# A DeltaNet scan whose matmuls are held in their written order, with counted bursts of projection matmuls between them

## The chip, the cores and the metric

The kernel runs on one core of one Trainium2 chip. The metric is the device time of one execution in microseconds. The median of the three runs shown of the kernel before is 1650.52 us (1648.81 to 1659.55). The execution that was profiled took 1652.23 us, and its trace spans 1650.5 us.

## What is computed

The reference is a trunk of two layers over 256 context tokens and 256 latent tokens of width 1024. In each layer a normalised input `h` goes through one wide projection, whose columns feed three mixers. They are a gated DeltaNet (A), a short convolution (B) and a neighbourhood attention (C). The mixers are gated, summed and projected, and a gated MLP follows. In the last layer only the latent tokens are carried on. The change lies where A and B meet.

A is a linear recurrence over chunks of 64 tokens, for four heads of width 128 and in both directions. The state of a direction at the end of the context starts its scan over the latent tokens:

```python
def step(S, inp):
    u_i, w_i, qk_i, qd_i, kd_i, gl_i = inp
    v_new = u_i - w_i @ S
    o_i = qd_i @ S + qk_i @ v_new
    S = S * gl_i + kd_i.T @ v_new
    return S, o_i
```

B is `bg * dwconv3(cg * hh)`, where `bg`, `cg` and `hh` are 512 columns each of the wide projection.

## The kernel before, in words

All tokens lie along the free axis: 512 columns in layer 0, and in layer 1 only the 256 latent columns where the context is not needed. A projection of 128 output columns is a sum of 24 matmuls (8 slices of the contraction, 3 products of high and low halves: `hi*hh`, `hi*hl`, `lo*hh`). Its weights are loaded by SP's queue, rounded to the high half by ScalarE (L192, `whi`), and the low half comes from a subtraction on VectorE (L195, `wlo`) or, for 24 tiles of layer 1, from a transfer of a half that was prepared before. The pools of `whi` and `wlo` hold three tiles in layer 0 and four in layer 1 (`WS`, L50).

**What is in a layer around the scan.** First come projections, convolutions and norms of k, v and q. VectorE then inverts small triangular blocks (L717 to L721), transposes the result (`Tl`, `Tf`, L722, L757 to L759), and TensorE completes the inverses with many 32x32 matmuls (`py` L772, `pz` L777), which ScalarE copies out (L773, L778). Then the scan runs: `s` = 0 is the context, `s` = 1 the latent tokens, each with four steps `n`. Both directions are worked together, one in each half of the partitions, and the four heads are worked as two groups of two. A step writes, in this order and each kind for both groups before the next kind:

- `pa<-S` (L888): k times the state; VectorE makes `rr` from it (L889)
- `pa<-wt` (L897): the inverse block times `rr`; ScalarE makes `vn` from it (L899)
- `po<-S` (L914): q times the state, where an output is wanted
- `pS` (L926): `kd` times `vn`; VectorE adds it to the decayed state `Sn` (L931)
- `po<-at` (L937): the second part of the output; VectorE adds it later (L944)

`build` (L824) prepares `wt` and `kd` of the next step on VectorE. The first step of a layer has no state, so it has neither `pa<-S` nor `po<-S`. The last has no `pS`.

**Where the short convolution comes in.** `short_conv` (L786) is a generator: it yields after each of its 288 matmuls (12 projections of 24, L792), and evacuates and convolves between projections. `fill(n)` (L815) advances it by `n * FILL[l][3]` matmuls. It is called after `pa<-S`, after `po<-S`, and, where no output is wanted, once more after `pS` (L890, L919, L950). What is left is written after the scan (L959).

**What sets the order.** The program is traced in written order, and a scheduler then orders each engine's instructions by its own estimate of times: of those that it takes as ready, the one written first goes first, so later work fills waits. `keep_in_program_order` ties an instruction behind the one that was traced just before it on its engine. With `SPIN[l]` = 0 neither the scan's matmuls nor those of `fproj` are tied.

Of the kernel before, what the change touches and what calls it, by code (L numbers as in the profile page):

```python
# [69 lines left out]
SQT, SQ0 = 4, 1  # L70
RQE, OTE, ATE, KDQ, KDC = (0, 0), 1, 0, 0, 0
BRO = (0, 1, 2)
SPIN = (0, 0)
FILL = ((3, 0, 0, 0), (0, 3, 2, 2))
UT = 0
QO = (0, 1)
LOE = ((0, 0, 3, 0), (4, 2, 3, 2))
# [7 lines left out]
def trunk(ctx, tc, xin, cin, cbin, con, par, w_ad0, w_ada, w_in, w_ab, bias, w_p, w_o, w_up, w_dn, out, dbg=None):  # L85
# [312 lines left out]
    for l in range(L):  # L398
# [387 lines left out]
        def short_conv():  # L786
            def fproj(ti):
                hi, lo = win(ti)
                ps = pbank("prj")
                for k in range(KD):  # L790
                    for i, (a, b) in enumerate(((hi, hh), (hi, hl), (lo, hh))):
                        mm = PE.matmul(ps[:, OW], a[:, k, :], b[:, k, NA_], start=k == 0 and i == 0, stop=k == KD - 1 and i == 2)  # L792
                        if in_scan[0]:
                            tc.keep_in_program_order(mm)
                        yield ps

            for i in range(4):
                cg = tmp("cg")
                for ps in fproj(SCT + 3 * i):
                    yield  # L800
                A.copy(cg[:, OW], ps[:, OW])
                for ps in fproj(SCT + 3 * i + 1):
                    yield
                uu = tmp("uu")
                V.tensor_tensor(uu[:, OW], ps[:, OW], cg[:, OW], ALU.mult)
                cv = tmp("cv")
                conv3(cv[:, OW].rearrange("p (s t) -> p s t", t=T), uu, lambda tap: pcol(l, "scc", tap * 4 + i), ns)
                for ps in fproj(SCT + 3 * i + 2):
                    yield
                V.tensor_tensor(y_b[:, i], ps[:, OW], cv[:, OW], ALU.mult)  # L810

        in_scan = [SPIN[l]]
        sc_gen = short_conv()

        def fill(n):  # L815
            for _ in range(n * FILL[l][3]):
                next(sc_gen, None)

        def mm(*a, **k):
            i_ = PE.matmul(*a, **k)  # L820
            if SPIN[l]:
                tc.keep_in_program_order(i_)
# [33 lines left out]
        for s in range(2):  # L856
            for n in range(4):
# [15 lines left out]
                for hs, gs in grp:  # L873
# [11 lines left out]
                    for i, h in enumerate(hs):  # L885
# [3 lines left out]
                        V.scalar_tensor_tensor(rr[:, i], pa[:, col2(i)], egr[:, c0 + h : c0 + h + 1], vpr[:, s, b, h], ALU.mult, ALU.subtract)  # L889
                fill(FILL[l][0])  # L890

# [12 lines left out]
                if want_o:  # L904
                    pos = []
                    for hs, gs in grp:
# [10 lines left out]
                        else:  # L917
                            pos[-1] = (po, None)
                fill(FILL[l][1] if want_o and S is not None else FILL[l][2])  # L919

# [28 lines left out]
                else:  # L949
                    fill(FILL[l][2])  # L950
                if not fin:
# [439 lines left out]
```

## Time and profile before

| | |
|---|---|
| median of three runs | 1650.52 us |
| profiled execution | 1652.23 us |
| its span | 1650.5 us |
| TensorE busy | 1588.7 us, 96% |
| VectorE busy | 1167.6 us, 71% |
| ScalarE busy | 799.6 us, 48% |
| GpSimd busy | 224.6 us, 14% |
| mean granted TensorE clock | 0.981 of full speed |

Ends of matmuls are modelled, so TensorE's busy share also holds short holes between instructions. The distance from one start to the next is the safer reading. The scan of layer 0 lies at about 163 to 226 us, that of layer 1 at about 1147 to 1207 us.

### The profile page before, as it was taken

The page shows a single profiled execution, that of the slowest core. Times are in us where ns is not written, and L with a number is a line of the kernel's source. Part 1 is how long each engine was busy: PE and PEld are TensorE (multiplying, and loading weights), DVE is VectorE, ACT ScalarE, POOL GpSimd, SP SyncE. Part 2 cuts the span into 40 slices and gives each one's busy share as a digit, 9 for nine tenths or more (in the row PEclk, how much of TensorE's full clock was granted, in tenths as well). Part 3 has the DMA queues.
Part 4 walks back from the last instruction along what each step waited for, and adds up shares of the span by engine and source line. Part 5 has one row for each costly group of instructions (what it writes and reads, how often), then busy time and mean ns, then how long its engine had stood idle before and what let it go on. Part 6 is the DMA issues. An engine that isn't in the chain of part 4 may idle for free. (4 is left out here: it accounts for less than half of the span.)

```text
span 1650.5 us, 26543 instructions
## 1 busy us (share of the span) xinstructions
PE 1588.7 (96%) x10184; PEld 1362.4 (83%) x10184; DVE 1167.6 (71%) x2311; ACT 799.6 (48%) x1409; POOL 224.6 (14%) x197
## 2 busy tenths in 40 slices
PE   5999999999799999999999999999999999999997
PEld 4677788877588888888888888788798899999997
DVE  3697763678788886878888776586757755677753
ACT  3764442656433333544444223574357554566653
POOL 0100310010000000000000000100332023334442
PEclk9998999999899999999999999997999999999999
DMA  9221012311676674365656876454134156645653
GB/s 372 78 65 52 27 39 90 109 61 43 199 239 230 235 238 139 115 204 178 207 184 195 279 251 203 176 174 171 52 99 128 56 181 183 188 152 181 188 172 112
DMA packets 75824, 257.80 MB, mean 156 GB/s; under 512 B 8433, under 2 KB 9841, under 8 KB 75569
## 3 DMA queue, kind: packets, MB, share of 16 engines
q1 hardware_dynamic: 71360, 239.37, 44.6%
q0 software_dynamic: 4336, 16.74, 2.8%
q8 instruction: 80, 1.31, 0.3%
q14 instruction: 48, 0.39, 0.1%
HBM read 242.44 MB, written 13.63 MB: 155 GB/s over the span
## 5 line engine op out<-in xcount | busy, mean ns | idle before, releaser
L192 ACT CAST whi<-wr 128x1024 fp32r<-128x1024 f32 (+2 forms) x312 | 288.2, 927 | 432.6 <-PE prj L206 99.7
L195 DVE TENSOR_TENSOR wlo<-wr,whi 128x512 fp32r<-128x512 f32 (+2 forms) x324 | 273.0, 859 | 124.2 <-ACT whi L192 118.8
L205 PE MATMUL prj<-hh,whi 128*128 128x512 f32 (+1 forms) x736 | 260.1, 353 | 5.2 <-ACT whi L192 2.0
L207 PE MATMUL prj<-hh,wlo 128*128 128x512 f32 (+1 forms) x736 | 260.0, 353 | 4.2 <-DVE wlo L195 4.2
L206 PE MATMUL prj<-hl,whi 128*128 128x512 f32 (+1 forms) x736 | 259.0, 352 | 0.0
L205 PE MATMUL pup<-hh,whi 128*128 128x256 f32 (+1 forms) x720 | 240.0, 335 | 1.4 <-ACT hh L370 1.4
L206 PE MATMUL pup<-hl,whi 128*128 128x256 f32 (+1 forms) x720 | 239.6, 334 | 0.0
L207 PE MATMUL pup<-hh,wlo 128*128 128x256 f32 (+1 forms) x720 | 239.5, 334 | 0.0
L195 POOL TENSOR_TENSOR wlo<-wr,whi 128x1024 fp32r<-128x1024 f32 (+2 forms) x72 | 142.7, 1983 | 300.4 <-ACT whi L192 289.6
L271 DVE SCALAR_TENSOR_TENSOR aprod<-araw,cb 128x1024 bf16<-128x1024 f32 x128 | 153.8, 1219 | 24.9 <-DMA araw<-w_ada 24.7
L205 PEld LDWEIGHTS prj<-hh,whi 128*128 128x128 f32 x736 | 139.7, 190 | 25.7 <-ACT whi L192 2.8
L207 PEld LDWEIGHTS prj<-hh,wlo 128*128 128x128 f32 x736 | 139.6, 190 | 23.7 <-DVE wlo L195 5.0
L206 PEld LDWEIGHTS prj<-hl,whi 128*128 128x128 f32 x736 | 139.6, 190 | 18.0 <-issue 1.9
L205 PEld LDWEIGHTS pup<-hh,whi 128*128 128x128 f32 x720 | 137.8, 192 | 15.1 <-ACT hh L370 2.0
L207 PEld LDWEIGHTS pup<-hh,wlo 128*128 128x128 f32 x720 | 137.7, 192 | 13.2
L206 PEld LDWEIGHTS pup<-hl,whi 128*128 128x128 f32 x720 | 137.5, 192 | 12.9
L206 PE MATMUL pdn<-fl,whi 128*128 128x256 f32 (+1 forms) x330 | 109.8, 333 | 0.0
L205 PE MATMUL pdn<-fh,whi 128*128 128x256 f32 (+1 forms) x330 | 109.7, 332 | 0.0
L207 PE MATMUL pdn<-fh,wlo 128*128 128x256 f32 (+1 forms) x330 | 109.7, 332 | 0.0
L164 POOL DMA_DIRECT2D lod<-araw x24 | 12.8, 532 | 520.8 <-DVE araw L162 520.8
L380 DVE SCALAR_TENSOR_TENSOR u<-pup,par,u 128x510 f32<-128x510 f32 (+1 forms) x88 | 53.6, 612 | 36.4 <-ACT u L379 36.4
L792 PE MATMUL prj<-hh,whi 128*128 128x512 f32 (+1 forms) x192 | 69.9, 364 | 0.0
(348 smaller groups left out, 3249.7 us busy)
## 6 DMA issues: line engine op xcount, KB each, us to landing
wr<-w_in SPq DMA_DIRECT2D x128, 512.0 KB, 4.1
wr<-w_up SPq DMA_DIRECT2D x88, 512.0 KB, 3.9
araw<-w_ada SPq DMA_DIRECT2D x80, 512.0 KB, 4.3
wr<-w_dn SPq DMA_DIRECT2D x32, 512.0 KB, 4.2
wr<-w_p SPq DMA_DIRECT2D x48, 256.0 KB, 2.9
araw<-w_in SPq DMA_DIRECT2D x24, 512.0 KB, 3.6
lod<-araw POOLq DMA_DIRECT2D x24, 512.0 KB, 3.2
wlo<-lod SPq DMA_DIRECT2D x24, 512.0 KB, 4.2
```

What stands on the lines that cost most here:

```text
L164: G.dma_start(lod[ti], raw)
L192: A.copy(hi[:, c], raw[:, c])
L195: E_.tensor_tensor(lo[:, c], raw[:, c], hi[:, c].bitcast(F32), ALU.subtract)
L205: PE.matmul(ps, hi[:, i, :], xh[:, i, n], start=first and i == 0, stop=False)
L206: PE.matmul(ps, hi[:, i, :], xl[:, i, n], start=False, stop=False)
L207: mm = PE.matmul(ps, lo[:, i, :], xh[:, i, n], start=False, stop=last and i == k - 1)
L271: V.scalar_tensor_tensor(prod, nxt, 1.0, cb[0][:, i], ALU.mult, ALU.mult, accum_out=macc[:, i, b : b + 1])
L380: V.scalar_tensor_tensor(dst[:, :, 1:T], pv[:, :, 0 : T - 1], wc(0), dst[:, :, 1:T], ALU.mult, ALU.add)
L792: mm = PE.matmul(ps[:, OW], a[:, k, :], b[:, k, NA_], start=k == 0 and i == 0, stop=k == KD - 1 and i == 2)
```

## The change

Both entries of `SPIN` become 1: the scan's matmuls (`mm`, L819) and those projection matmuls that `fill` draws while the scan is written (L793) are each tied behind the matmul traced before them. Those that are drawn after the scan stay free. `FILL` gets new counts: in layer 0 a step draws 2 x 3 = 6 projections after `pa<-S` and 1 x 3 = 3 after `po<-S` (or in its place). In layer 1 it draws 3 x 3 = 9 after `pa<-S`, then 2 x 3 = 6 twice in a context step, and 1 x 3 = 3 in a latent step.

```diff
-SPIN = (0, 0)
-FILL = ((3, 0, 0, 0), (0, 3, 2, 2))
+SPIN = (1, 1)
+FILL = ((2, 1, 1, 3), (3, 1, 2, 3))
```

## Rows read from the trace of the kernel before

**Rows 1.** The page, busy time of each engine.
```profile
PE 1588.7 (96%) x10184; PEld 1362.4 (83%) x10184; DVE 1167.6 (71%) x2311; ACT 799.6 (48%) x1409; POOL 224.6 (14%) x197
```

**Rows 2.** Windows, layer 0: stretch, length, busy and count per engine, clock, DMA.
```profile
125.60:163.20 37.60, 37.11 (x407) 26.99 (x405) 28.66 (x66) 15.28 (x23) 0.00 (x0) 0.89 0.13 39
172.40:221.60 49.20, 47.91 (x403) 36.09 (x402) 39.84 (x109) 24.97 (x66) 16.06 (x26) 1.00 0.04 12
226.50:268.30 41.80, 41.80 (x186) 34.61 (x186) 19.70 (x26) 11.69 (x15) 1.43 (x2) 1.00 0.27 88
```

**Rows 3.** Windows of L792 alone: before, in and after each scan.
```profile
125.60:163.20 37.60, 21.57 (x74) 14.09 (x73) 0.89 0.13 39
163.20:226.50 63.30, 13.67 (x31) 6.54 (x31) 0.96 0.08 24
226.50:268.30 41.80, 41.80 (x184) 34.42 (x184) 1.00 0.27 88
1109.50:1147.50 38.00, 20.75 (x150) 19.19 (x150) 0.83 0.61 212
1147.50:1207.00 59.50, 18.77 (x72) 12.16 (x72) 0.97 0.14 45
1207.00:1215.00 8.00, 7.96 (x66) 7.98 (x66) 1.00 0.06 7
```

**Rows 4.** The timeline of VectorE, layer 0 before the scan.
```profile
135.48 1.22 DVE L195 TENSOR_TENSOR wlo<-wr,whi 128x1024 fp32r<-128x1024 f32 x1
...
140.87 0.17 DVE L576 COPY cols<-psst 128x16 f32<-128x16 f32 x1 [0.86 <-PE psst L573]
...
160.21 1.23 DVE L195 TENSOR_TENSOR wlo<-wr,whi 128x1024 fp32r<-128x1024 f32 x1
```

**Rows 5.** The timeline of TensorE, layer 0 before the scan.
```profile
151.71 0.80 PE L792 MATMUL prj<-hh,whi 128*128 128x512 f32 x1
...
154.99 2.01 PE L772 MATMUL py<-ax,X 32*32 32x32 f32 x61
...
160.70 0.80 PE L792 MATMUL prj<-hl,whi 128*128 128x512 f32 x1
```

**Rows 6.** The chain that ended last, layer 1 before the scan.
```profile
1125.44 1.63 PE prj L792 x12
...
1135.37 2.00 PE prj L792 x8
...
1145.29 0.51 PE prj L792
```

**Rows 7.** The timeline of TensorE in the scan of layer 0.
```profile
172.44 0.66 PE L820 MATMUL pa<-S,k__507 128*64 128x128 f32 x8
...
181.03 0.50 PE L792 MATMUL prj<-hh,whi 128*128 128x512 f32 x1
181.46 0.66 PE L820 MATMUL pa<-S,k__507 128*64 128x128 f32 x8
181.94 0.60 PE L820 MATMUL po<-S,q__501 128*64 128x128 f32 x6
...
185.33 1.77 PE L820 MATMUL pS<-vn,kd 64*128 64x128 f32 x14
187.04 1.16 PE L820 MATMUL po<-vn,at 128*128 128x128 f32 x8
188.13 0.66 PE L820 MATMUL pa<-S,k__507 128*64 128x128 f32 x8
...
221.62 0.66 PE L820 MATMUL pa<-S,k__507 128*64 128x128 f32 x8
```

**Rows 8.** The timeline of TensorE, starts of steps in the scan of layer 1.
```profile
1154.63 0.44 PE L820 MATMUL pa<-S,k__9172 128*64 128x128 f32 x4
...
1177.72 0.54 PE L820 MATMUL pa<-S,k__9172 128*64 128x128 f32 x5
...
1202.12 0.44 PE L820 MATMUL pa<-S,k__9172 128*64 128x128 f32 x4
```

## The prediction

> **What bounds the kernel now.** I read the busy shares first: TensorE is busy for 96% of the span and nothing else comes near [rows 1]. So a matmul costs nothing only where TensorE would wait, and the question is where such places are and what fills them. The windows by stage show it. After the scan of layer 0, TensorE is busy for all of 41.80 us, VectorE for less than half [rows 2]: what is added there lengthens the kernel. Before the scan TensorE also looks full, but the windows of line 792 alone show that 21.57 of its 37.11 busy us are short-convolution projections, work written later that was moved up. What is left there is a chain: VectorE's block inverses and transposes, TensorE's `py` and `pz`, ScalarE's copies.
>
> So I count where the 288 projection matmuls of each layer run [rows 3]. In layer 0, 74 lie before the scan, 31 in it and 184 after it (one straddles two windows). In layer 1 it is 150, 72 and 66. The ones before the scan are almost free now. In the scan the timeline shows steps of about 8 us in which lone projections stand between the scan's matmuls [rows 7].
>
> **What the change does to these places.** The tie is to the matmul traced just before, so the first tied projection stands behind the last `pz`, and the others behind the scan's matmuls. Thus 72 matmuls of layer 0 (8 steps of 9) and 132 of layer 1 (4 x 21 and 4 x 12) can no longer run before the scan. Could the free ones written later take their place? Their weights need a place among three (layer 0) or four (layer 1) tiles, and the first three or four projections, written first, hold them until the scan uses them. The trace agrees that three are prepared ahead: the third `wlo` of these runs at 135.48, the fourth only at 160.21, after the first had been used [rows 4]. So I take the stretch before the scan as empty of projections.
>
> **Term 1, after the scan.** Layer 0 keeps 288 - 72 = 216 there instead of 184: 32 more at 41.80/184 = 0.227 us [rows 3] are **+7.3 us**. Layer 1 keeps 156 instead of 66: 90 at 7.96/66 = 0.121 us are **+10.9 us**. Nothing hides this, as TensorE is full there.
>
> **Term 2, before the scan.** The projections that leave also stood in the way. In layer 0 seven of them run from 151.71 to 154.99 ahead of the third `py`, 3.3 us, and another takes 0.8 before the last `pz` [rows 5]. VectorE waits 0.86 us for `psst`, which projections delay [rows 4]. Sum 5.0. In layer 1 the chain itself runs through 1.63, 2.00 and 0.51 us of them [rows 6], sum 4.1. I take the whole, **-9.1 us**. Late next would be what these matmuls wait for themselves (copies by ScalarE), so the other end is 0.
>
> **Term 3, the scan.** For a step in written order I add prices from one step [rows 7]. `pa<-S` has 16 records; eight take 0.48 (181.46 to 181.94), so 0.96, and the same for `po<-S`. `pS`: 14 in 1.71, so 1.95 for 16. `po<-at`: 1.09 for 8, and I give `pa<-wt`, of the same shape, the same. That is 6.05 us. Nine projections at 0.227 are 2.04. A lone projection between half-width matmuls holds TensorE for 0.43 (181.03 to 181.46), 0.2 more than in a stream; I charge that 0.2 once per burst, two bursts, 0.4. Sum **8.5 us**, where the six middle steps now take (221.62 - 172.44)/6 = 8.2: +1.8. The first step now takes 9.2 (163.2 to 172.44). Projections there run at 0.47 each (3.28/7, half clock), nine are 4.2, and with 1.09, 1.95, 1.09 and 0.4 it is 8.7: -0.5. The last lacks `pS`, 6.55 against 226.5 - 221.62 = 4.9: +1.7. Layer 0: **+3.0 us**.
>
> Layer 1: a context step is 0.96 + 1.09 + 1.95 + 21 x 0.121 + 3 x 0.2 = 7.1, against (1177.72 - 1154.63)/3 = 7.7 [rows 8]: three save 1.7. A latent step is 6.05 + 12 x 0.121 + 0.4 = 7.9 against 8.1: three save 0.7. The first adds 0.2 (nine projections at twice 0.121), the last 1.1 (5.95 against 4.9). Layer 1: **-1.1 us**.
>
> Why no further stall: the six or nine projections behind `pa<-S` cover `rr`, `po<-S` with the three behind it covers `vn`, and `po<-at` covers the last add into the state. If that cover is too thin, what follows in written order waits with it, as nothing tied may pass; that is rival A. VectorE is busy 39.84 of 49.2 us in the middle steps [rows 2], 6.6 of 8.2 per step, so it stays below 8.5. Bounds for a step: 0.6 less (the 0.2 per burst gone and `pa<-wt` 0.2 cheaper), or 1.0 more (rival A). I take the sum, being nearest to rows of the same matmuls.
>
> **Two things of no or unknown cost.** `fill` also moves the evacuations (L801 to L810) and the weight loads on SP's queue later, with the matmuls that they serve. SP is no bound: DMA shares are 0.04 to 0.28 in these stretches [rows 2]. ScalarE is busy for half. I cost them at nothing; if a weight load is late, a burst waits and the scan with it, up to one load per projection, again rival A.
>
> The clock: the granted clock is 0.89 in the stretch before the scan of layer 0 and 0.83 in layer 1 [rows 3], with projections keeping TensorE at work. Without them it may stay at the lower level (1.2 GHz) for the `pss`, `psst` and `gram` matmuls. I take 0 and keep as the other end 2 us per layer, an estimate from the 0.86 us that VectorE now waits for `psst`, doubled and rounded up. The Trainium skill (TensorE: Matmul & The Clock Gate, "Part 1: The HAM clock gate") says that the gate's default is the halved rate and that activity releases it. That speaks against the change; by it the sum would be the one with the 4 us.
>
> **The sum.** 7.3 + 10.9 - 9.1 + 3.0 - 1.1 = **+11.0 us** on the profiled execution's 1652.2: 1663.2. That execution lies 1.7 above the median, so I forecast **1662 us**, which is +0.7% on 1650.5. A measurement of this kernel tells about 1% (16.5 us) from no change.
>
> **Rivals.**
> A, *the tied scan stalls* (slower). VectorE or ScalarE issues something long ahead of `rr`, `vn` or a state add, such as a `wlo` of 1.23 us [rows 4] that itself waits for its `whi`. Before, TensorE took another matmul in that time; now all behind waits. At 1.0 us in each of 14 middle and edge steps it is +14: 1676. It decides from about 0.4 us per step, where the total passes 1%. For it: VectorE has only 1.9 us to spare per step. Against: the order kind by kind leaves cover at each wait.
>
> B, *the stretch before the scan stays full*. If the free projections do get places, term 1 (18.2) and term 2 (-9.1) both vanish: 1652.2 + 1.9, less 1.7, is 1652. For it: the scheduler's order is not seen in the trace. Against: the three `wlo` ahead.
>
> C, *the changes of shape are the loss*. Steps are 0.6 us shorter than my sum, 14 x 0.6 = 8.4: 1653. With B as well, and with nothing stalled, 1644. The lone projection's 0.43 against 0.227 speaks for it. The Trainium skill (TensorEngine Tiling (Array Packing), "Key Properties") has as a rule that changing the tiling mode drains the engine. By that rule sorting the kinds is worth more than I charge, and the total would be C's; the trace agrees that a change costs 0.2, but much of that is already in the steps that I compare with.
>
> D, *the change doesn't bind*: free projections still slip between the tied matmuls, so the bursts are longer or broken, and the scan takes as long as now with the rest unchanged: 1651. Against: ties hold by construction; only what is free can slip in.
>
> **Chances.** Forecast 0.45, A 0.27, B 0.10, C 0.13, D 0.05. The forecast's own range is 1655 to 1671 (term 2 at half, the clock's 4). Slower by over 1% (above 1667): most of A and a seventh of the forecast, 0.29. Faster by over 1% (below 1634) would need B, C and more, 0.08. Within 1%: 0.63. The range 1646 to 1678 holds all but the far ends of A and of B with C.
>
> **What would show it.** Right: no line-792 matmul between the last k, v, q work and the last `pz`, except after it; about 216 and 156 of them after the scans; steps near 8.5, 7.1 and 7.9 us; the scans starting 5 and 4 us earlier within their layers. Wrong: line-792 matmuls before the scan as now (B); TensorE idle inside the scan put down to VectorE or ScalarE (A); steps below 8 us with nine projections (C). The prediction falls if the projections lost before the scan are found somewhere that costs nothing.

## The result: 6% slower, and the profile after

The changed kernel takes 1748.15 us (median of six runs, 1742.75 to 1759.73) against 1650.42 us: a ratio of 1.0597 (95% interval 1.057 to 1.0624). The forecast was 1662 us with a range up to 1678, so it was wrong by far, on the side of rival A. The profiled execution is the slowest of the six, 1759.73 us. Its span is 1757.9 us, 107.4 us longer than before, where the medians differ by 97.7.

The page first: the busy line and the row of granted clocks in 40 slices.

```profile
PE 1641.7 (93%) x10184; PEld 1396.3 (79%) x10184; DVE 1169.0 (66%) x2311; ACT 801.5 (46%) x1409; POOL 228.7 (13%) x197
...
PEclk9997569999989999999999999986779999999999
```

The counts are those of [rows 1]; VectorE and ScalarE do the same work in the same time. TensorE alone is busy for 53 us more, and the clock is low in two places, slices 4 to 6 and 27 to 30. These are the two scans with the stretches just ahead of them. The windows of line 792 alone, cut before, in and after each scan, answer to [rows 3] (length, TensorE busy and count, weight loads, clock, DMA):

```profile
126.00:160.00 34.00, 0.00 (x0) 0.00 (x0) 0.64 0.08 25
160.00:287.00 127.00, 48.00 (x128) 27.53 (x128) 0.71 0.05 15
287.00:324.20 37.20, 36.55 (x161) 29.96 (x160) 1.00 0.34 107
1165.70:1197.80 32.10, 0.00 (x0) 0.00 (x0) 0.57 0.16 56
1197.80:1305.50 107.70, 31.99 (x149) 26.37 (x149) 0.69 0.15 49
1305.50:1322.80 17.30, 16.84 (x139) 16.73 (x139) 1.00 0.66 220
```

No projection runs before a scan any more, as forecast. But the scans now take 127 and 108 us where they took 63.3 and 59.5 [rows 3], at a mean clock of 0.71 and 0.69. The waits of TensorE say for what it sat idle (us in total, times, longest):

```profile
PE pa L820 <- ACT vn L899: 13.6, 24, 1.1
PE pa L820 <- DVE rr L889: 11.0, 24, 0.5
...
PE po L820 <- ACT oacc L915: 3.8, 8, 0.5
PE po L820 <- ACT ot L915: 2.9, 6, 0.5
```

None of these rows is in the profile before, but for one wait of 0.4 us. A context step of layer 1 at the full clock, in TensorE's timeline, shows where they sit (the bracket is idle time before the row, and its releaser):

```profile
1222.87 0.44 PE L820 MATMUL pa<-S,k__9172 128*64 128x128 f32 x4
1223.76 0.66 PE L820 MATMUL pa<-S,k__9172 128*64 128x128 f32 x8 [0.46 <-DVE rr L889]
1224.91 0.44 PE L820 MATMUL pa<-S,k__9172 128*64 128x128 f32 x4 [0.49 <-DVE rr L889]
...
1226.46 0.38 PE L820 MATMUL pa<-rr,wt 128*128 128x128 f32 x2
1227.94 0.71 PE L820 MATMUL pa<-rr,wt 128*128 128x128 f32 x4 [1.10 <-ACT vn L899]
1229.17 0.49 PE L820 MATMUL pa<-rr,wt 128*128 128x128 f32 x2 [0.52 <-ACT vn L899]
...
1233.33 0.44 PE L820 MATMUL pa<-S,k__9172 128*64 128x128 f32 x4
```

Four records are one head. Head 0 runs, then TensorE waits until VectorE has made `rr` of head 0; heads 1 and 2 run together, and head 3 waits for the `rr` of head 2. Heads 0 and 1 write into one bank of the accumulation memory, and so do 2 and 3. Between the two, the code has the evacuation of the first, that is, the read that takes its result out of the bank. VectorE's own timeline has that read from 1223.35, for 0.35 us, and head 1 starts at 1223.76. Head 0 needs about 0.24 us of issue, and head 1 starts 0.89 after it. `pa<-wt` has the same two waits for `vn`, and `po<-S` for `ot`: four waits in a context step of layer 1, six in every step with an output. The one of 1.10 us is longer because ScalarE, until 1227.54, still worked off a `whi` (1.05 us from 1226.18) and a `cv` that were issued ahead of `vn`.

The Trainium skill (PSUM — Partial Sum Buffer, "PSUM bank collisions raise a hardware error") says that two engines may not touch one bank in the same partitions at once, even at different columns, and that this must be guarded by semaphores. The waits in the trace fit that: the two heads write different columns, and yet the second starts only after the read of the first has ended (1223.70, then 1223.76).

In the steps with outputs the clock is low as well. Windows of all engines:

```profile
180.00:190.00 10.00, 9.10 (x45) 6.87 (x44) 4.39 (x11) 0.81 (x2) 2.78 (x4) 0.50 0.00 0
260.00:270.00 10.00, 10.00 (x65) 6.79 (x63) 3.29 (x7) 4.03 (x10) 1.08 (x2) 1.00 0.07 12
```

At 180 us the granted clock is 0.50, the 1.2 GHz level, and a step takes 19.6 us (185.38 to 205.00 in the timeline, against 8.2 before). From about 250 us free projections have got places for their weights and fill the waits. The clock is back, but a step still takes 14.8 us (260.39 to 275.20), with 30 projections in it. They stand in eight bursts; by the forecast's prices that is 6.05 + 30 x 0.227 + 8 x 0.2 = 14.5 us.

### The profile page after: what moved, and what is told of

Same layout as the page of the kernel before. It is cut to its first block, busy times and chain, and to the rows that moved or that the text cites. A ratio compares the mean times of both kernels' runs of the same rounds, so it can differ in the third digit from the quotient of the medians.

```text
span 1757.9 us, 26559 instructions
## 1 busy us (share of the span) xinstructions
PE 1641.7 (93%) x10184; PEld 1396.3 (79%) x10184; DVE 1169.0 (66%) x2311; ACT 801.5 (46%) x1409; POOL 228.7 (13%) x197
## 5 line engine op out<-in xcount | busy, mean ns | idle before, releaser
L205 PE MATMUL prj<-hh,whi 128*128 128x512 f32 (+1 forms) x736 | 260.2, 354 | 4.5 <-ACT gt L1115 1.5
L792 PE MATMUL prj<-hh,whi 128*128 128x512 f32 (+1 forms) x192 | 77.0, 401 | 0.0
```

The lines of the kernel that those rows point to most:

```text
L205: PE.matmul(ps, hi[:, i, :], xh[:, i, n], start=first and i == 0, stop=False)
```

## The experiments

Three theories stood. **W**: the two heads of a group share a bank, the tie leaves the waits between them empty, and the clock falls with them. **P**: the emptied stretch before the scan and the moved projections are the loss. **T**: holding the order is itself the loss. Ratios are to the kernel before, run on the same chip.

**e1_fill_only**, the counts alone:

```diff
-FILL = ((3, 0, 0, 0), (0, 3, 2, 2))
+FILL = ((2, 1, 1, 3), (3, 1, 2, 3))
```

> The new counts of FILL alone, nothing tied. Theory W (two heads of a group share one accumulation bank, so in written order the second head's matmuls wait for VectorE or ScalarE to read the first; the tie leaves these waits empty, and TensorE then also loses its clock): without the tie the waits are filled by whatever is ready, so about as before, 1640 to 1662 us. Theory P (the counts move the projections out of the stretch before the scan, and that emptied stretch starts the loss of the clock): projections are written inside the scan, but free ones still move up, so also near before; only if the counts themselves cost would it be above 1690 us.

1649.47 us, ratio 0.9994 (0.9979 to 1.001). Without a tie the counts are worth nothing, either way.

**e2_tie_only**, the tie alone:

```diff
-SPIN = (0, 0)
+SPIN = (1, 1)
```

> The tie alone, with the old FILL: in layer 0 no projection is tied (count 0), in layer 1 56 are. W: in layer 0 all 288 projections stay free and fill the stretch before the scan and the waits in it, so layer 0 costs 0 to 8 us; in layer 1 the tied steps keep waits that free projections can fill only once places for weights come free: 1655 to 1690 us in all. Rival T (holding the order is itself the loss, whatever fills it): about the changed kernel's 1748, 1725 to 1765 us.

1711.76 us, ratio 1.0373 (1.0345 to 1.0402). Neither theory's number was met: W's bound was too low by 22 us, T's by 13 too high. The windows of the two scans tell why:

```profile
163.00:262.00 99.00, 97.92 (x640) 68.39 (x639) 58.47 (x140) 38.26 (x90) 22.21 (x32) 0.97 0.13 41
1145.00:1253.00 108.00, 91.61 (x472) 69.62 (x473) 37.78 (x107) 23.45 (x59) 17.95 (x26) 0.54 0.08 27
```

In layer 0 no projection is tied. Free ones fill the waits (one of 0.3 us is left), TensorE is full at a clock of 0.97, and the last projection of the short convolution starts only 2.9 us later than before (270.98 against 268.10). In layer 1 the 56 tied ones hold back the others: waits stay empty, the clock is 0.54, and the scan takes 108 us. From the last projection of q to the last of line 792, layer 0 takes 3 us longer than before and layer 1 takes 59. So the tie costs little where free work fills the waits and about what it costs in the change where it doesn't. That is W in kind; T would have layer 0 slow too.

**e3_split_tied**, the changed kernel with the evacuations behind both heads (the same edit for `vn` and for `ot`):

```diff
                     for i, h in enumerate(hs):
                         for d in range(2):
                             t0 = s * T + chunks[d] * C
                             mm(pa[halves[d], col2(i)], k_[:, h, t0 : t0 + C], S[:, h, d], start=True, stop=True)
+                    for i, h in enumerate(hs):
                         V.scalar_tensor_tensor(rr[:, i], pa[:, col2(i)], egr[:, c0 + h : c0 + h + 1], vpr[:, s, b, h], ALU.mult, ALU.subtract)
```

> The changed kernel, ties and counts kept, but the three evacuations (rr, vn, and ot or oacc) are written after the matmuls of both heads of a group instead of between them, so that no matmul of a kind waits for a read of its own bank. Nothing is left out. W: no waits inside a kind, steps near 8.5 us in layer 0 and 7.1 and 7.9 in layer 1, the clock stays up in the scan, 1652 to 1675 us (the sum of the prediction was 1662). P: the stretch before the scan is as empty as in the changed kernel and the clock still falls there and stays down, so 1715 us or more. T: 1735 us or more.

1662.92 us, ratio 1.0075 (1.006 to 1.009): 85 us of the 98 are gone, with ties, counts and the emptied stretch before the scan kept. A step of layer 0 in TensorE's timeline:

```profile
166.59 1.09 PE L820 MATMUL pa<-S,k__507 128*64 128x128 f32 x16
...
169.10 1.05 PE L820 MATMUL pa<-rr,wt 128*128 128x128 f32 x8
170.09 1.09 PE L820 MATMUL po<-S,q__501 128*64 128x128 f32 x16
...
172.00 2.00 PE L820 MATMUL pS<-vn,kd 64*128 64x128 f32 x16
173.94 1.16 PE L820 MATMUL po<-vn,at 128*128 128x128 f32 x8
175.02 1.09 PE L820 MATMUL pa<-S,k__507 128*64 128x128 f32 x16
```

Each kind runs through all four heads without a stop, and the step takes 8.43 us. The windows of line 792 show the same counts as the forecast, and the clock:

```profile
124.00:157.90 33.90, 0.00 (x0) 0.00 (x0) 0.68 0.07 26
157.90:223.00 65.10, 22.77 (x72) 13.42 (x72) 0.96 0.05 17
223.00:272.60 49.60, 49.16 (x216) 40.47 (x216) 1.00 0.31 96
1145.60:1203.00 57.40, 22.03 (x132) 18.00 (x132) 0.96 0.29 93
```

The clock before the scan is as low as in the changed kernel (0.68 and 0.64), yet the scan runs at 0.96. So the empty stretch isn't what holds the clock down inside the scan. The changed kernel says so too: its first scan ran at 1.00 from 164 to 174 us, and the clock fell after that. P falls.

**e4_split_free**, the same three edits on the kernel before:

> The kernel before (nothing tied, old FILL) with the same three evacuations written after both heads' matmuls. W: the waits inside a kind, which free matmuls fill only in part, are gone; steps of layer 0 fall from 8.2 towards 7.5 us, 1636 to 1650 us. P and T: no effect, 1647 to 1654 us.

1641.41 us, ratio 0.9942 (0.9922 to 0.9962). The edit is worth some 9 us without a tie too, although the waits were filled. From the first `pa<-wt` to the start of the last piece of `po<-at`, the scan of layer 0 goes from 58.8 us to 50.4. That is not all gain: 18 fewer projections run in it, and the stretch behind it grows by 3.5 us (42.5 to 46.0).

**e5_split_tied_fill0**, e3 with all projections free:

```diff
-FILL = ((2, 1, 1, 3), (3, 1, 2, 3))
+FILL = ((0, 0, 0, 0), (0, 0, 0, 0))
```

> The scan tied as in the change, the evacuations written after both heads' matmuls, and all counts of FILL zero, so that all 288 projections of a layer stay free. Theory W (the waits inside a kind are the loss; the projections that leave the stretch before the scan cost what terms 1 and 2 of the prediction say): no such waits, and the stretch before the scan is full again, so below the 1663 of the tied kernel with counts: 1635 to 1652 us. Theory T (holding the order costs by itself): above 1665 us, since nothing written covers the latencies of rr and vn.

1635.21 us, ratio 0.9903 (0.987 to 0.9935), the fastest of all. Line 792 before and in the first scan, and before and in the second:

```profile
124.20:163.30 39.10, 23.64 (x82) 15.84 (x82) 0.92 0.16 49
163.30:216.50 53.20, 11.68 (x32) 5.30 (x32) 1.00 0.07 21
...
1097.20:1137.80 40.60, 23.41 (x162) 21.90 (x162) 0.82 0.57 199
1137.80:1186.00 48.20, 11.99 (x56) 7.89 (x55) 0.98 0.14 45
```

82 and 162 projections are back ahead of the first `pa<-wt`, as many as in the kernel before by the same bounds. The tie costs nothing here (untied, in e4, the ratio is 0.9942), so T falls. Against e3 the counts, that is, tying 72 and 132 projections, cost 1.7% (1.0075 less 0.9903), some 28 us; that much of P is right.

**e6_alternate**, the changed kernel with the heads in the order 0, 2, 1, 3, each evacuation still right behind its head (shown for the start of `pa<-S`, the rest left out; `vn` and `ot` alike):

```diff
-                    for i, h in enumerate(hs):
+                for i in range(2 if S is not None else 0):
+                    for (hs, gs), pa, rr in zip(grp, pas, rrs):
+                        h = hs[i]
                         for d in range(2):
```

> The changed kernel, ties and counts kept and each evacuation still written right behind its head's matmuls, but in each kind the heads alternate between the two groups (0, 2, 1, 3 in place of 0, 1, 2, 3), so that two neighbours never share a bank. If the shared bank makes the wait (W), head 2 runs in head 0's wait and one exposed wait per kind is left in place of two: a step of the context in layer 1 at the full clock falls from 10.4 to about 8.9 us, and 1675 to 1715 us in all, depending on whether the clock holds. If a written evacuation between matmuls makes the wait, whatever the bank (W'), three waits per kind and no gain: 1740 us or more.

1687.89 us, ratio 1.0215 (1.0189 to 1.0242). A context step of layer 1:

```profile
1171.03 0.66 PE L820 MATMUL pa<-S,k__9172 128*64 128x128 f32 x8
1171.93 0.70 PE L820 MATMUL pa<-S,k__9172 128*64 128x128 f32 x8 [0.24 <-DVE rr L891]
...
1173.73 0.61 PE L820 MATMUL pa<-rr,wt 128*128 128x128 f32 x4
1174.73 0.75 PE L820 MATMUL pa<-rr,wt 128*128 128x128 f32 x4 [0.39 <-ACT vn L903]
...
1179.15 0.66 PE L820 MATMUL pa<-S,k__9172 128*64 128x128 f32 x8
```

Heads 0 and 2 run together although an evacuation is written between them; head 1 then waits, less long, and head 3 hardly. One wait per kind is left in place of two, and the step takes 8.1 us in place of 10.4, less than the 8.9 expected. The shared bank makes the wait, not the evacuation as such. (Bank and tile are one thing in this program, `gbank`, L130, so no run tells a wait for the bank from a wait for the tile.)

**e7_fill_at_waits**, the changed kernel with the same number of tied projections per step, drawn where the second head waits:

```diff
                         V.scalar_tensor_tensor(rr[:, i], pa[:, col2(i)], egr[:, c0 + h : c0 + h + 1], vpr[:, s, b, h], ALU.mult, ALU.subtract)
-                fill(FILL[l][0])
+                        if i == 0:
+                            fill(0, hs[0] // 2, s)
```

(the rest left out: alike behind the first `vn` and `ot` of a group; 2 and 2, 2 and 1, 1 and 1 projections in a step of layer 0 but its first, 5 and 5, 5 and 6 in a context step and 2 everywhere in a latent step of layer 1).

> The changed kernel, ties kept, evacuations where they were, and the same number of projections tied into each step (9 in layer 0, 21 and 12 in layer 1), but drawn after the first head of each group, where the second head waits, instead of between kinds. W: most of each wait of about 0.7 us (from the end of one head's issue to the next) is covered by one to six projections, what is left is 1 to 2 us per step, and TensorE keeps its clock: 1665 to 1700 us. P or T (the number of tied projections, the emptied stretch before the scan, or the order of kinds is the loss): as the changed kernel, above 1730 us.

1697.33 us, ratio 1.0291 (1.0247 to 1.0334). In a context step of layer 1 the waits between heads are covered, all but one:

```profile
1181.78 0.44 PE L820 MATMUL pa<-S,k__9172 128*64 128x128 f32 x4
...
1182.93 0.66 PE L820 MATMUL pa<-S,k__9172 128*64 128x128 f32 x8
...
1185.16 0.44 PE L820 MATMUL pa<-S,k__9172 128*64 128x128 f32 x4 [0.79 <-DVE rr L890]
...
1190.22 0.44 PE L820 MATMUL pa<-S,k__9172 128*64 128x128 f32 x4
```

The step is 8.4 us, and the scans run at clocks of 0.97 and 0.98. The same projections, tied, cost 50 us less when they stand where the waits are. e3 is faster by another 34 us: e7 keeps 19 waits for `rr`, `vn` and `oacc` of 8.7 us together, and its TensorE is busy 24 us longer with the same matmuls. How much of that are the changes between projections and scan matmuls was not measured.

## Why the prediction was wrong, point by point

The starts of the stages in TensorE's timeline give each term of the sum its measure: from the last projection of q to the first `pa<-wt`, from there to the last `po<-at` (its first record), and from there to the last projection of line 792. A burst of projections of the first step lies ahead of the first `pa<-wt`; counted to the last `pz`, as the forecast's terms are, the stretches ahead of the scans shrink by 3.9 and 5.9 us and the scans of e3 differ by +2.3 and -1.7.

| stage, us | before | changed | e3 | forecast of the difference | changed - before | e3 - before |
|---|---|---|---|---|---|---|
| layer 0, ahead of the scan | 41.4 | 36.6 | 36.6 | -5.0 | -4.8 | -4.8 |
| layer 0, scan | 58.8 | 124.2 | 62.0 | +3.0 | +65.4 | +3.2 |
| layer 0, after it | 42.5 | 37.0 | 49.7 | +7.3 | -5.5 | +7.2 |
| layer 1, ahead of the scan | 40.9 | 34.3 | 34.3 | -4.1 | -6.6 | -6.6 |
| layer 1, scan | 55.9 | 105.2 | 54.8 | -1.1 | +49.3 | -1.1 |
| layer 1, after it | 8.7 | 17.4 | 19.6 | +10.9 | +8.7 | +10.9 |
| sum | | | | +11.0 | +106.5 | +8.8 |

**Where the projections go** was right: none before the scans, and in e3 216 and 156 after them, as counted. In the changed kernel fewer are left for after (161 and 139), because free ones filled waits late in the scans; that is part of its scan's length. With these counts rival B falls, and D as well, but for those late free ones.

**Term 2** was right in kind: 4.8 us where 5.0 were forecast, and 6.6 where 4.1 were. The projections did stand in the chain's way. The 2 us per layer kept for the clock were not needed: the stretches became shorter although their clock fell from 0.89 to 0.68 and from 0.83 to 0.54 in e3. The 6.6 are not safe: e1, with the same 162 projections there, takes 37.0 us ahead of the scan of layer 1 at a clock of 0.95, against 40.9 at 0.83 in the execution before.

**Term 1** was right where no wait took projections into the scan: +7.2 and +10.9 in e3. That e3 as a whole lands so near the forecast (1662.92 against 1662) is in part luck, since the first row of layer 1 is off by 2.5 us.

**Term 3 failed**, and in it one sentence: "Why no further stall". It listed the latencies between kinds (`rr`, `vn`, the state add) and found cover for each, and e3 shows that this cover holds: its steps of 8.43 us stand against 8.5. It did not look inside a kind. The program writes head 0, its evacuation, head 1, its evacuation, and both heads share a bank. With the tie, six evacuations per step stand in TensorE's way. In the trace before they are not seen as waits, since free matmuls ran in their place:

```profile
172.44 0.66 PE L820 MATMUL pa<-S,k__507 128*64 128x128 f32 x8
172.98 0.44 PE L820 MATMUL po<-S,q__501 128*64 128x128 f32 x4
173.34 0.50 PE L792 MATMUL prj<-hh,whi 128*128 128x512 f32 x1
173.78 0.44 PE L820 MATMUL po<-S,q__501 128*64 128x128 f32 x4
174.05 0.39 PE L820 MATMUL pa<-S,k__507 128*64 128x128 f32 x4
```

The lone projection and the alternation of `pa` and `po`, that I read as a disorder costing changes of shape, were this filling. Rival A named the right symptom (VectorE or ScalarE late, all behind waits, "nothing tied may pass") but not its place, and its price of 1.0 us per step was a fraction of the real one: 10.4 us against the forecast 7.1 in a context step of layer 1, 19.6 against 8.5 in a step of layer 0 at the low clock. What A describes, a long instruction ahead of `vn`, is there too, but small: the 1.10 us wait above.

**The clock inside the scans** was missing from the sum. The prediction weighed it only ahead of them and took 0; the scans then ran at 0.71 and 0.69.

How the +65.4 us of layer 0 divide can only be estimated. e3 differs from the changed kernel by the places of the evacuations alone, and its scan of layer 0 is 62.2 us shorter. Of these, 12.7 are projections that e3 runs behind the scan (49.7 less 37.0). The trace of the changed kernel has 28 waits for evacuations in this scan; at 0.65 us each (0.89 from head to head, less the head's own 0.24) they make 18. That leaves some 31 us to the low clock and, in the last steps, the changes of shape. A single step shows the same: of the 19.62 us from 185.38 to 205.00, TensorE is busy for 16.72 and idle for 2.90, where e3's whole step takes 8.43. The busy line of e3's page:

```profile
PE 1573.6 (95%) x10184; PEld 1359.8 (82%) x10184; DVE 1166.4 (70%) x2311; ACT 793.5 (48%) x1409; POOL 228.0 (14%) x197
```

Over the whole execution, TensorE of the changed kernel is busy 68.1 us longer than e3's with the same matmuls, and idle 30.4 us longer. So the waits themselves are the smaller part of the loss; the clock that falls with them seems to be the larger.

That the low clock belongs to the empty waits, and not to the empty stretch before, three runs show: the same stretch with the waits gone, 0.96 (e3); the same stretch with the waits covered, 0.97 and 0.98 (e7); a tied scan whose waits free projections fill, 0.97 (e2, layer 0). The Trainium skill (TensorE: Matmul & The Clock Gate, "A second HAM failure mode: psum-queue depth-cycling") tells of a kernel whose many short idle moments between groups of matmuls kept the clock moving between its levels. Here it moved too, but stayed low for longer: 0.50 from 178 to 209 us, a mean of 0.81 from 209 to 214, then 0.51 to 252. What exactly lets it fall stays open: in the changed kernel it was 1.00 from 1222 to 1250 us with four waits in a step, and in e6, which keeps about half the waits, it is 0.94 and 0.98 in the scans.

**Rival C** (changes of shape are the loss) has no support as a gain over the forecast: a tied step by kind took the 8.5 us that the sum gives.

One slip changes nothing: the DMA shares of [rows 2] reach 0.27, not 0.28, and they are of layer 0 alone; ahead of the scan of layer 1 the share is 0.61 [rows 3].

## What to carry to other kernels

When a tie takes away an engine's freedom, read the written order instruction by instruction for what the freedom was hiding: any read by another engine that is written between two matmuls into one bank became a wait here. Write the evacuations behind all matmuls of the bank, and tie only after that; here that turns 1748 us into 1663 with the same ties, and 1635 with the filling left free. Work that fills a chain-bound stretch earlier on should not be tied into a later one, which cost 28 us.

## What was not expected of the hardware

From 178 to 209 us and from 214 to 252 us TensorE was at the 1.2 GHz level (0.50 and 0.51) while the trace calls it 87% busy, and from 1222 to 1250 us it ran at 1.00 while 72% busy. The busy share of a profile did not tell the clock; closing or covering the waits brought it back.

A wait inside a kind makes 0.89 us from one head's start to the next. Of these, 0.48 pass before VectorE starts to read (1222.87 to 1223.35), the read takes 0.35, and 0.06 pass until the next head starts.

In e7 a tied burst of five projections of 256 columns covers the first such wait fully, but the second only in part (0.79 us left). VectorE's timeline shows why: before the `rr` of the middle heads, from 1184.50, it worked on `wt` and `kd` of the next step from 1182.81, the last of them 0.69 us long.
